# Sixteen experts in eight pairs of 64 slots, by plain float32 matmuls on weights as they come from memory

## The chip, the core and the metric

One core of a Trainium2 chip runs one program: a block with a state-space mixer, attention and a mixture of experts, and behind it a block of two layers with three kinds of attention, cross-attention and a feed-forward part. The metric is the device time of one execution in microseconds, as the median of runs. The engines named here are TensorE (PE in the profile; PEld is its loading of stationary operands), VectorE (DVE), ScalarE (ACT), GpSimd (POOL) and SyncE (SP), which issues nearly all loads.

## The reference

Only the mixture of experts matters. There are 256 tokens of 1024 features, four groups of four experts with 512 hidden features each, and all of it is float32. A token goes to the two best experts of its best group.

```python
g_prob = softmax(t @ w_rg + b_rg); g_p, g_idx = top_k(g_prob, 1)
e_in = (logits of the four experts of that group)
top_l, top_i = top_k(e_in, 2); w_k = softmax(top_l) * g_p
for e in range(16):
    hid = silu(t @ w_gate[e]) * (t @ w_up[e])       # [256, 1024] @ [1024, 512]
    out = out + gates[:, e:e+1] * (hid @ w_down[e])  # [256, 512] @ [512, 1024]
x = layer_norm(ALPHA * x + (1 + gt2) * out, ln2_g, ln2_b)
```

The weights of the experts are 16 x 3 matrices of 1024 x 512 float32, 2.10 MB each.

## The kernel before

Every large product takes float32 operands as two parts of type float32r, a higher and a lower one, and makes three matmuls of them (`mm3`, lines 159 to 163: high by high, high by low, low by high). Activations are split once. Weights come through `raw` (line 113: a buffer of 8 KB per partition, six in turn, loaded on SP's queue), and `wparts1` (line 128) splits them: a cast by ScalarE to the higher part and a subtraction by VectorE to the lower part, both in `split` at line 226, into two sets of four buffers of 4 KB (`hi` and `lo`).

`moe` (line 1038) norms the tokens, transposes and modulates them (`h2T`), and makes the router's logits (`plog`, line 1057; `lg`, line 1067). VectorE picks group and experts by a chain of small operations. The ranks of the tokens in their group come from matmuls with a strictly triangular matrix (line 1074), and from the ranks a one-hot matrix `S` of tokens by slots, 128 slots for each of the four groups (line 1094). Expert 0 takes every token, which gives TensorE work while the slots are made (`linB`, then `linA` with `dense`, lines 1130 to 1165). A branch for a group with more than 128 tokens stands between these two.

`gather` (line 1212) multiplies the normed tokens with `S`, so that each slot gets its token, feature-major. `experts` (line 1268) then goes through fifteen jobs, one for each remaining expert, each over the 128 slots of its group: gate and up (`pgu`, 24 matmuls each), silu and product (lines 1306 and 1307), four transposes (line 1322), and down (`yg`, 24 matmuls). A group's sum is brought back to its tokens by `combine` (line 1351) with the transposed one-hot matrix. The gate of the next expert is written between the steps of the one before. Which instruction comes when on each engine is set by a scheduler before the run, in order of the source as far as operands are there by its reckoning; on the chip each engine keeps that order. `after` puts instructions behind given ones.

Behind the experts follow a layer norm and the second block. Keys and values of its second memory (`keys`, `values`) fill TensorE during that norm. The first memory's values (`self.values(0, ...)`) fill the router's time.

Of the kernel before, what the change touches and what calls it, by code (L numbers as in the profile page):

```python
# [16 lines left out]
P = 128  # L17
# [37 lines left out]
KCST = NCST - 4 * P     # without the identity in front and the masks behind  # L55


def bc(ap, axis, n):
    """insert a broadcast dimension of n at axis"""
    u = ap.unsqueeze(axis)  # L60
    shape = list(u.shape)
    shape[axis] = n
    return u.to_broadcast(shape)


class Build:
# [75 lines left out]
    def wblk(self, src, a, b, r=None, pages=None):  # L142
        """a block of weights [128, a, b], split into its two parts: pairs of [128, b]. r: loaded before"""
# [7 lines left out]
    def wpages(self, src, a, b):  # L151
        """the same by way of pages alone; and these, to be freed"""
# [63 lines left out]
    def linB(self, x, KT, W, n0, r=None, w=None):  # L216
        """feature-major (x @ W[:, n0:n0+256])^T: a bank [128, 2, 256]"""
# [10 lines left out]
    # feature-major activations in two parts: pages of four feature tiles [128, 4, 256]  # L228
# [11 lines left out]
    def featT(self, src, KT, xT, t):  # L240
        """transpose the token-major src [128, KT*128] of token tile t into xT"""
# [10 lines left out]
    def rsq(self, src, mul, eps, n, name):  # L252
        """(src*mul + eps) ** -0.5"""
# [13 lines left out]
    def square(self, sq, n, x, out=None):  # L267
        """half n of the sum of squares of x [128, 1024]; sq: a page for the squares, a column for each half"""
# [8 lines left out]
    def rms1(self, sq, r):  # L277
        """r = (the mean of the squares + eps) ** -0.5"""
# [6 lines left out]
    def norm1(self, sq, x, g, r=None):  # L285
        """the page of sq gets the rms-normed x with its gain"""
# [7 lines left out]
    def normT(self, x, gain, name, sq=None, eng=None, r=(None, None)):  # L294
        """rms-normed x with its gain, transposed, in two parts. sq: the squares, where they are summed already"""
# [7 lines left out]
        self.chain = []     # the splits, in their order  # L303
# [28 lines left out]
    def lngb(self, out, v, st, g, b, then):  # L332
        """out = layer norm of v with gain and bias, by halves; then(n): called after each"""
# [40 lines left out]
    def ptile(self, pr, nh, n, eng):  # L374
        """the nh*n transposes [128 keys, nh, n, 128 queries] of the probabilities pr [128, nh, n*128]"""
# [13 lines left out]
    def attn(self, qk, V, out, first=True, nsink=None, gate=None, swa=False):  # L389
        """Causal attention of four heads over 256 tokens, added to out [128, 2, 256] (pairs of heads on  # L390
# [317 lines left out]
    def mixer1(self):  # L708
# [155 lines left out]
        for m in mods:  # L864
            self.modend(m)
# [987 lines left out]
```

## Time and profile before

| | |
|---|---|
| median of three runs | 1766.82 us (1764.88 to 1770.11) |
| the profiled execution, from its first to its last instruction | 1764.4 us |
| TensorE busy | 1686.6 us (96%) |
| VectorE busy | 1216.9 us (69%) |
| ScalarE busy | 940.7 us (53%) |
| read from memory | 337.85 MB, 192 GB/s over the span |
| router, first expert, fifteen experts, tail of the experts | 381 to 718 us |

A busy TensorE is not one at its peak: matmuls overlap, and their ends are modelled. What a matmul costs in a stream is the distance from one start to the next, not its duration.

### The profile page before, as it was taken

To read this page: it belongs to the slowest core of one execution; us is meant where nothing else is said; L and a number is where in the kernel's file an instruction comes from. 1 tells how busy PE (TensorE), PEld (TensorE's weight loads), DVE (VectorE), ACT (ScalarE), POOL (GpSimd) and SP (SyncE) were. 2 spreads that over 40 slices of the span, in tenths; PEclk is the share of its full clock that TensorE was granted. 3 is DMA by queue.
4 is the path that set the end of the run, shared out by engine and by line. 5 is a ranking of instruction groups with operands and counts; after the bars stand their busy time and mean duration, and the time that the engine had idled before them with its cause. 6 is when DMAs were issued, how large, how long until landed. Compare 5 with 4: busy or idle time off the path is not lost. (4 is left out here: it accounts for less than half of the span.)

```text
span 1764.4 us, 25175 instructions
## 1 busy us (share of the span) xinstructions
PE 1686.6 (96%) x9802; PEld 1420.9 (81%) x9818; DVE 1216.9 (69%) x1724; ACT 940.7 (53%) x1497; POOL 233.4 (13%) x260
## 2 busy tenths in 40 slices
PE   6699999999999999999999999999999999999998
PEld 5579888887888877786778779998777778789986
DVE  6856875886899988777754765554677746755543
ACT  3346754455777776566554455443575544544442
POOL 3589245120000000200000000000100000000000
PEclk9699999989999999999999999999999999999999
DMA  9867366545899989453335635654453255535550
GB/s 313 293 199 229 96 227 238 167 168 163 314 312 370 354 316 367 147 190 88 114 114 188 205 108 179 196 181 150 140 170 98 72 168 202 182 129 173 186 191 24
DMA packets 206845, 340.60 MB, mean 193 GB/s; under 512 B 19792, under 2 KB 99776, under 8 KB 206720
## 3 DMA queue, kind: packets, MB, share of 16 engines
q1 hardware_dynamic: 202864, 331.29, 56.0%
q0 software_dynamic: 1936, 6.52, 1.1%
q8 instruction: 79, 1.29, 0.3%
q10 hardware_dynamic: 1920, 1.11, 0.2%
q14 instruction: 46, 0.38, 0.1%
HBM read 337.85 MB, written 1.05 MB: 192 GB/s over the span
## 5 line engine op out<-in xcount | busy, mean ns | idle before, releaser
L226 DVE TENSOR_TENSOR wlo<-raw,whi 128x1024 fp32r<-128x1024 f32 (+3 forms) x560 | 680.0, 1232 | 340.3 <-ACT whi L226 334.5
L226 ACT CAST whi<-raw 128x1024 fp32r<-128x1024 f32 (+3 forms) x560 | 568.8, 1031 | 461.8 <-PE psA L163 167.3
L161 PE MATMUL psB<-hTh,whi 128*128 128x256 f32 x896 | 255.3, 285 | 0.9 <-DVE xbc L859 0.9
L163 PE MATMUL psB<-hTh,wlo 128*128 128x256 f32 x896 | 255.1, 285 | 0.8 <-DVE wlo L226 0.8
L162 PE MATMUL psB<-hTl,whi 128*128 128x256 f32 x896 | 255.3, 285 | 0.0
L161 PE MATMUL psA<-whi,hTh 128*128 128x512 f32 (+4 forms) x496 | 187.9, 379 | 2.6 <-ACT sg L950 1.9
L163 PE MATMUL psA<-whi,hTl 128*128 128x512 f32 (+4 forms) x496 | 187.4, 378 | 0.5 <-DVE hTl L226 0.5
L162 PE MATMUL psA<-wlo,hTh 128*128 128x512 f32 (+4 forms) x496 | 186.3, 376 | 0.0
L161 PEld LDWEIGHTS psB<-hTh,whi 128*128 128x128 f32 x896 | 171.6, 192 | 3.7 <-DVE xbc L859 1.8
L162 PEld LDWEIGHTS psB<-hTl,whi 128*128 128x128 f32 x896 | 171.3, 191 | 1.9 <-issue 1.9
L163 PEld LDWEIGHTS psB<-hTh,wlo 128*128 128x128 f32 x896 | 171.4, 191 | 1.7 <-DVE wlo L226 1.1
L161 PEld LDWEIGHTS psA<-whi,hTh 128*128 128x128 f32 x496 | 93.7, 189 | 20.8 <-ACT sg L950 2.3
L163 PEld LDWEIGHTS psA<-whi,hTl 128*128 128x128 f32 x496 | 93.5, 188 | 19.0 <-issue 2.4
L162 PEld LDWEIGHTS psA<-wlo,hTh 128*128 128x128 f32 x496 | 93.6, 189 | 16.1 <-issue 0.7
L162 PE MATMUL pgu<-wlo,gh 128*128 128x512 f32 x240 | 96.0, 400 | 2.2 <-DVE wlo L226 2.0
L361 ACT ACTIVATE pr<-S,nm 128x256 f32<-128x256 f32 (+1 forms) x160 | 66.3, 425 | 59.5 <-DVE nm L354 41.8
L161 PE MATMUL pgu<-whi,gh 128*128 128x512 f32 x240 | 95.6, 399 | 0.0
L163 PE MATMUL pgu<-whi,gl 128*128 128x512 f32 x240 | 94.7, 395 | 0.0
L633 POOL TENSOR_TENSOR macc<-macc,wmod 128x512 f32<-128x512 f32 x59 | 92.6, 1571 | 1.8
L162 PE MATMUL pd<-wlo,hhl 128*128 128x512 f32 x176 | 69.7, 396 | 0.0
L163 PE MATMUL pd<-whi,hhl 128*128 128x512 f32 x176 | 69.5, 395 | 0.0
L161 PE MATMUL pd<-whi,hhl 128*128 128x512 f32 x176 | 69.2, 395 | 0.0
(595 smaller groups left out, 3248.1 us busy)
## 6 DMA issues: line engine op xcount, KB each, us to landing
raw<-in_w_in SPq DMA_DIRECT2D x62, 1024.0 KB, 5.1
raw<-in_w_down SPq DMA_DIRECT2D x52, 1024.0 KB, 5.9
raw<-in_w_gate_up SPq DMA_DIRECT2D x44, 1024.0 KB, 5.1
raw<-in_w_gate SPq DMA_DIRECT2D x32, 1024.0 KB, 6.4
raw<-in_w_up SPq DMA_DIRECT2D x32, 1024.0 KB, 6.5
wmod<-in_w_mod SPq DMA_DIRECT2D x48, 512.0 KB, 5.5
raw<-in_w_xkv SPq DMA_DIRECT2D x8, 1024.0 KB, 9.6
raw<-in_w_out SPq DMA_DIRECT2D x8, 1024.0 KB, 5.0
```

Of the source, the lines that this page charges most:

```text
L161: m(out, l[0], r[0], start=start, stop=False)
L162: m(out, l[0], r[1], start=False, stop=False)
L163: self.lastmm = m(out, l[1], r[0], start=False, stop=stop)
L226: return self.nc.scalar.copy(hi, src), self.nc.vector.tensor_sub(lo, src, hi.bitcast(F32))
L361: le = nc.scalar.activation(pr[:, h, :], S[:, h, :], AF.Exp, bias=nm[:, h:h + 1], accum_out=den[:, h:h + 1])
L633: return e.tensor_add(acc, acc, w)
```

## The change

An expert has 64 slots instead of a group 128. Ranks and one-hot matrix are made for each of the 16 experts, after the choice of experts. Two experts make a pair. Expert 2q has the first 64 columns of TensorE's array and expert 2q + 1 the last 64, so that their results stand on partitions 0 to 63 and 64 to 127 of one PSUM bank. The operands are plain float32: the weights are used as they are loaded, without parts. Features are assigned to partitions in another order, partition p holding features 8p to 8p + 7, so that a partition reads 8 KB of a weight matrix in one piece; the modulation of the second norm, the transposes and the router's weights follow that order. A chunk of weights (1 MB) goes to a `raw` buffer or to a pair of `hi` and `lo` buffers in turn. All sixteen experts go this way, expert 0 too. If an expert has more than 64 tokens, a branch between pairs 3 and 4 multiplies all tokens by all experts with the gates of those that found no slot. The second memory's load and the first split of its weights are issued behind the last load of the experts.

The diff, cut to its core:

```diff
+    CHUNKS = "rrhrh"
+    def wchunk(self, src):
+        n, b = src.shape[1:]
+        kind = self.CHUNKS[self.nchunk % len(self.CHUNKS)]
+        self.nchunk += 1
+        if kind == "r":
+            r = self.raw(src, n, b)
+            return [r[:, k * b:(k + 1) * b] for k in range(n)]
+        out = []
+        for h, tag in enumerate(("hi", "lo")):
+            m = n // 2
+            t = self.wp.tile([P, 1024], F32, tag=tag, bufs=self.HL, name="wx")
+            v = t.rearrange("p (a b) -> p a b", a=m)
+            self.lastraw = self.nc.sync.dma_start(v, src[:, h * m:(h + 1) * m, :])
+            out += [v[:, k, :] for k in range(m)]
+        return out
...
+            nc.tensor.matmul(pk[:, t * 16:t * 16 + 16], self.stri, sf[:, t, :], start=True, stop=t == 0, skip_group_check=True)
+        nc.tensor.matmul(pk[:, 16:32], self.ones, sf[:, 0, :], start=False, stop=True, skip_group_check=True)
...
+            nc.vector.tensor_tensor(Sp[t].rearrange("p (e s) -> p e s", e=16), bc(self.iota[:, 0:64], 1, 16), bc(rr[:, t, :], 2, 64), op=ALU.is_equal)
...
+        for b in range(2):
+            for k in range(8):
+                ps = self.bank("o" if k % 2 else "tp", "pga")
+                for t in range(2):
+                    r = Sp[t][:, b * 512:(b + 1) * 512]
+                    for n, v in enumerate((xh, xl)):
+                        nc.tensor.matmul(ps, v[t].rearrange("p (q k) -> p k q", k=8)[:, k, :], r, start=t == 0 and n == 0, stop=t == 1 and n == 1)
...
-        W = [A[n][0, 0] for n in ("w_gate", "w_up", "w_down")]
-        hid = [self.glu(self.linB(self.T(h2), 8, W[0], b * 256), self.linB(self.T(h2), 8, W[1], b * 256)) for b in range(2)]
...
-        self.experts(jobs, acc, st=st, ahead=first, early=early, more=pair(1), fin=mem)
+        wgu = lambda j, e, c: W[j][e].rearrange("(p k) n -> p k n", k=8)[:, 4 * c:4 * c + 4, :]
+        wdn = lambda e, c: W[2][e].rearrange("(p j) n -> p j n", j=4)[:, 2 * c:2 * c + 2, :]
+        def half(q, j):
+            ps = self.bank("lin", "pgu")
+            for c in range(2):
+                w = ready.pop(0) if ready else [self.wchunk(wgu(j, 2 * q + i, c)) for i in range(2)]
+                for k in range(4):
+                    kt = 4 * c + k
+                    for i in range(2):
+                        x = xg[q // 4][kt // 2][:, kt % 2, q % 4 * P + i * 64:q % 4 * P + i * 64 + 64]
+                        self.lastmm = nc.tensor.matmul(ps[i * 64:i * 64 + 64, :], x, w[i][k], start=kt == 0, stop=kt == 7, skip_group_check=True)
+            return ps
...
+        for q in range(8):
+            if q == 4:
+                ready += [[self.wchunk(wgu(0, 8 + i, c)) for i in range(2)] for c in range(2)]
+                self.overflow(oi, hT, gov, acc)
+                self.f(*hT, *xgp[0])
+            pg, pu = half(q, 0), half(q, 1)
+            if late:
+                self.combine(ST[(q - 1) // 4][:, (q - 1) % 4, :], evac(late), acc)
+            hid = self.a(2, "hid")
+            nc.scalar.activation(hid, pg, AF.Silu)
+            nc.vector.scalar_tensor_tensor(hid, hid, gs[:, q:q + 1], pu, op0=ALU.mult, op1=ALU.mult)
+            pt = v4(self.bank("m", "pth"))
+            for k in range(4):
+                nc.tensor.transpose(pt[:, k, :], hid.rearrange("p (f k) -> p k f", k=4)[:, k, :], self.ident)
+            hx = self.a(2, "hx")
+            nc.scalar.copy(v4(hx), pt)
+            y = [self.bank("S", f"yg{n}") for n in range(2)]
+            for c in range(2):
+                w = [self.wchunk(wdn(2 * q + i, c)) for i in range(2)]
+                for k in range(2):
+                    for n in range(2):
+                        for i in range(2):
+                            nc.tensor.matmul(y[n][i * 64:i * 64 + 64, :], v4(hx)[:, 2 * c + k, i * 64:i * 64 + 64], w[i][k][:, n * 512:(n + 1) * 512],
+                                             start=c == 0 and k == 0, stop=c == 1 and k == 1, skip_group_check=True)
+            self.f(hid, hx)
+            late = y
+        with self.after(self.lastraw):
+            mT = self.memT(1)
+            w = self.wB(8, A["w_xkv_2"][1], 0)
+        self.combine(ST[1][:, 3, :], evac(late), acc, st)
...
+    def overflow(self, oi, hT, gov, acc):
+        flag = nc.values_load(oi[0:1, 0:1], min_val=0, max_val=1)
+        with self.tc.If(flag > 0):
+            for e in range(16):
...
+                                nc.tensor.matmul(ps[t], v4(hT[k // 4])[:, k % 4, t * P:(t + 1) * P], wv[:, k - k0, :], start=k == 0, stop=k == 7)
```

## Rows read from the trace of the kernel before

**Rows 1.** The page: busy time, share of the span and instructions of each engine.
```profile
PE 1686.6 (96%) x9802; PEld 1420.9 (81%) x9818; DVE 1216.9 (69%) x1724; ACT 940.7 (53%) x1497; POOL 233.4 (13%) x260
```
**Rows 2.** Windows: stretch, length; PE, PEld, DVE, ACT, POOL busy; clock, DMA share, GB/s.
```profile
340.00:381.00 41.00, 37.90 (x171) 31.39 (x170) 33.34 (x45) 16.88 (x27) 14.65 (x12) 0.79 0.42 138
381.00:427.00 46.00, 41.68 (x289) 38.46 (x289) 31.30 (x79) 24.43 (x31) 0.00 (x0) 0.96 0.53 176
427.00:704.00 277.00, 274.01 (x1231) 219.61 (x1229) 251.82 (x266) 205.88 (x230) 2.24 (x4) 1.00 0.93 332
...
440.00:460.00 20.00, 20.00 (x90) 16.11 (x89) 18.30 (x17) 15.35 (x17) 0.00 (x0) 1.00 0.71 256
```
**Rows 3.** Stationary loads for gate and up's PSUM tile: ns min/median/max.
```profile
L161 PEld LDWEIGHTS pgu<-whi,gh x240: 187/188/192, 427.0 to 689.3; 128*128 128x128 f32 x120
```
**Rows 4.** Waits of the SP queue, 430 to 705 us: total, times, longest.
```profile
SPq L116 <- DVE wlo L226: 226.7, 81, 8.8
```
**Rows 5.** Groups of instructions, 427 to 704 us: busy us, mean ns.
```profile
L226 DVE TENSOR_TENSOR wlo<-raw,whi 128x1024 fp32r<-128x1024 f32 x172 | 203.9, 1221 | 15.3 <-ACT whi L226 13.9
L226 ACT CAST whi<-raw 128x1024 fp32r<-128x1024 f32 x173 | 177.9, 1051 | 50.4 <-PE pgu L163 28.6 <-PE yg L163 18.5 <-ACT hf L1229 0.6
...
L1307 DVE SCALAR_TENSOR_TENSOR hid<-hid,gs,pgu 128x512 f32<-128x512 f32 x15 | 11.1, 743 | 0.2 <-PE pgu L163 0.2
```
**Rows 6.** Timeline, a plain float32 matmul of attention scores: start, us, instruction.
```profile
811.33 1.02 PE L424 MATMUL S<-kaD,qaT 128*128 128x512 f32 x2
```
**Rows 7.** Timeline, the attention's value products, 64 columns wide.
```profile
795.56 0.27 PE L414 MATMUL oT<-PT,vm 128*64 128x128 f32 x1
795.57 0.27 PE L413 MATMUL oT<-PT,vm 128*64 128x128 f32 x1
795.67 0.27 PE L415 MATMUL oT<-PT,vm 128*64 128x128 f32 x1
```
**Rows 8.** DMA view of three saturated windows: 92 to 100, 66 to 76, 601 to 607 us.
```profile
DMA packets 2767, 2.79 MB, mean 348 GB/s; under 512 B 46, under 2 KB 2767, under 8 KB 2767
...
DMA packets 2000, 3.86 MB, mean 386 GB/s; under 512 B 116, under 2 KB 116, under 8 KB 2000
...
DMA packets 738, 2.43 MB, mean 405 GB/s; under 512 B 45, under 2 KB 45, under 8 KB 737
```
**Rows 9.** Timeline of the router: VectorE's chain, TensorE's ranks, ScalarE's last copy of values.
```profile
378.78 0.59 ACT L1711 COPY vx<-psA 128x512 f32<-128x512 f32 x1 [0.55 <-PE psA L163]
...
382.07 0.19 DVE L1067 TENSOR_TENSOR lg<-plog,rb 128x40 f32<-128x40 f32 x1
...
383.50 0.17 DVE L1026 TENSOR_TENSOR oh<-lg,gm 128x8 f32<-128x8 f32 x1
...
384.10 0.17 DVE L1030 TENSOR_TENSOR oh<-oh,ohm 128x8 f32<-128x8 f32 x1
...
384.42 0.57 PE L1074 MATMUL prank<-oh,cst 128*128 128x4 f32 x4
...
385.70 0.17 DVE L1079 SCALAR_TENSOR_TENSOR rr<-prank,oh 128x8 f32<-128x8 f32 x1 [0.97 <-PE prank L1077]
```
**Rows 10.** Timeline of TensorE: the gates of the slots and the transposed one-hot.
```profile
422.69 0.95 PE L1242 MATMUL pgs<-wg,S 128*128 128x4 f32 x8
423.50 0.42 PE L1250 MATMUL pst<-idt,S 128*128 128x128 f32 x2
```
**Rows 11.** Timeline of TensorE at the branch, and the window behind it.
```profile
409.88 0.47 PE L161 MATMUL psA<-whi,hhl 128*128 128x512 f32 x1 [4.12 <-PEq L1144]
...
410.00:415.00 5.00, 5.00 (x16) 3.93 (x17) 0.53 (x1) 0.00 (x0) 0.00 (x0) 0.66 0.63 203
```
**Rows 12.** Timeline of the tail: the last expert matmul, a split, the last statistics.
```profile
701.99 0.39 PE L163 MATMUL yg<-whi,hl 128*128 128x512 f32 x1
...
707.88 1.22 DVE L226 TENSOR_TENSOR wlo<-raw,whi 128x1024 fp32r<-128x1024 f32 x1
...
716.34 1.28 DVE L312 BATCH_NORM_STATS2 bst<-acc 128x6 f32<-128x512 f32 x2
```

More of the change, by code (lines that the diff above doesn't have):

```diff
@@ L672, in mod, with modendq @@
         return list(self.modsteps(j))[-1]
+    def modendq(self, ja):
+        j, acc = ja
+        ps = self.bank("m", "psmod")
+        mm = self.nc.tensor.matmul
+        mm(ps[:, 0:8], self.ident, self.bq[:, j - 3, :], start=True, stop=False, skip_group_check=True)
+        for k in range(8):
+            mm(ps[:, k:k + 1], acc.rearrange("p (q k) -> p k q", k=8)[:, k, :], self.ones[:, 0:1], start=False, stop=True, skip_group_check=True)
+        if j == 4:
+            self.nc.vector.tensor_scalar(self.modq[:, 1, :], ps[:, 0:8], 1.0, None, op0=ALU.add)
+        else:
+            self.nc.scalar.copy(self.modq[:, 0, :], ps[:, 0:8])
+        self.f(acc)
     def modend(self, ja):
@@ L863, in mixer1 @@
         Bf, Cf = v4(xp[2]), v4(xp[3])
[L864 to L865 removed]
+        self.modend(mods[0])
+        self.modendq(mods[1])
         with self.after(self.lastraw):
@@ new lines, in moe @@
+        ov = self.small([P, 2, 16], "ov", 1)
+        nc.vector.tensor_scalar(ov, rr, 63.5, None, op0=ALU.is_ge)
+        of = self.small([P, 1], "of", 1)
+        nc.vector.tensor_reduce(of, ov.rearrange("p t e -> p (t e)"), axis=AX.X, op=ALU.add)
+        pf = self.bank("o", "pof")
+        nc.tensor.matmul(pf[:, 0:1], self.ones, of, start=True, stop=True)
+        oi = self.cp.tile([1, 1], I32, name="oi")
+        nc.vector.tensor_scalar(of[0:1], pf[0:1, 0:1], 1.0, None, op0=ALU.min)
+        nc.vector.tensor_copy(oi, of[0:1])
@@ new lines, in moe @@
+        self.behind = self.behind0
+        self.values(0, self.mT0)
+        self.freeT(self.mT0)
+        Sf = [v.bitcast(F32) for v in Sp]
+        pg = self.bank("m", "pgs")
+        for q in range(8):
+            for t in range(2):
+                nc.tensor.matmul(pg[:, 2 * q:2 * q + 2], Sf[t][:, q * P:(q + 1) * P], g16[:, t, 2 * q:2 * q + 2], start=t == 0, stop=t == 1,
+                                 skip_group_check=True)
+        gs = self.small([P, 8], "gs", 1)
+        for i in range(2):
+            c = slice(i * 64, (i + 1) * 64)
+            nc.vector.tensor_copy(gs[c, :], pg[c, 0:16].rearrange("p (q i) -> p q i", i=2)[:, :, i])
@@ new lines, in moe @@
+        STp = [self.a(4, f"ST{i}", F32R) for i in range(2)]
+        ST = [v4(v) for v in STp]
+        for i in range(2):
+            for t in range(2):
+                pt = v4(self.bank("m", "pst"))
+                for q in range(4):
+                    nc.tensor.transpose(pt[:, q, :], Sf[t][:, (4 * i + q) * P:(4 * i + q + 1) * P], self.ident)
+                nc.scalar.copy(ST[i][:, :, t * P:(t + 1) * P], pt)
+        xg = [[self.a(4, f"xg{b}{i}").rearrange("p (a b) -> p a b", a=2) for i in range(4)] for b in range(2)]
@@ L1130, in moe @@
         self.mod_tm(5, gt)
-        self.behind = self.behind0
-        self.values(0, self.mT0)
-        self.freeT(self.mT0)
-        W = [A[n][0, 0] for n in ("w_gate", "w_up", "w_down")]
-        hid = [self.glu(self.linB(self.T(h2), 8, W[0], b * 256), self.linB(self.T(h2), 8, W[1], b * 256)) for b in range(2)]
-        self.freeT(h2)
-        ahead = [self.raw(W[2][:, n * 512:(n + 1) * 512].rearrange("(k p) n -> p k n", p=P), 4, 512) for n in range(2)]
-        first = [self.raw(*self.wsrc(A[n][0, 1], k0)) for n in ("w_gate", "w_up") for k0 in (0, 4)]
@@ L1186, in moe @@
-        list(pair(0))
-        st = self.newst()
-        mT, w = [], []
-        def mem():
-            with self.after(self.lastraw):
-                mT.extend(self.memT(1))
-                w.extend(self.wB(8, A["w_xkv_2"][1], 0))
-        self.experts(jobs, acc, st=st, ahead=first, early=early, more=pair(1), fin=mem)
+        st = self.newst()
+        self.nchunk = 0
+        W = [A[n][0] for n in ("w_gate", "w_up", "w_down")]
+        wgu = lambda j, e, c: W[j][e].rearrange("(p k) n -> p k n", k=8)[:, 4 * c:4 * c + 4, :]
@@ L1235, in slots @@
-    def slots(self, S, wg, ng):
-        nc = self.nc
-        Sf = S.bitcast(F32)
-        pg = self.bank("m", "pgs")
-        for g in range(ng):
-            for t in range(2):
-                nc.tensor.matmul(pg[:, g * 4:g * 4 + 4], Sf[:, t, g, :], wg[:, t, :], start=t == 0, stop=t == 1)
-        gs = self.small([P, ng, 4], "gs")
-        nc.vector.tensor_copy(gs, pg[:, 0:4 * ng].rearrange("p (a b) -> p a b", a=ng))
-        STp = self.a(ng, "ST", F32R)
-        ST = STp.rearrange("p (g t) -> p g t", g=ng)
-        for t in range(2):
-            pt = self.bank("m", "pst").rearrange("p (a b) -> p a b", a=4)
-            for g in range(ng):
-                nc.tensor.transpose(pt[:, g, :], Sf[:, t, g, :], self.ident)
-            nc.scalar.copy(ST[:, 0:ng, t * P:(t + 1) * P], pt[:, 0:ng, :])
-        return gs, STp
@@ L1362, in combine, with glu @@
         self.f(*y[0], *y[1])
+    def glu(self, pg, pu):
+        h = self.a(2, "hid")
+        hv = h.rearrange("p (a b) -> p a b", a=2)
+        self.nc.scalar.activation(hv, pg, AF.Silu)
+        self.nc.vector.tensor_mul(hv, hv, pu)
+        hl = self.a(4, "hhl", F32R)
+        self.split(hl[:, 0:512], hl[:, 512:1024], h)
+        self.f(h)
+        return hl
     def rope(self, dst, src, t, H, w=64):
```

295 lines of the change are left out of this document (105 added, 190 removed).

## The prediction

> **What bounds the kernel now.** I read the page's shares first, then a table of windows around the mixture of experts, then single instructions. TensorE is busy for 96% of the span [rows 1], so at first sight it is the bound everywhere. The table of windows [rows 2] divides the part that changes: the router and the first, dense expert (381 to 427 us), fifteen experts of 128 slots (427 to 704 us) and the tail (704 to 718 us). In the 277 us of the experts TensorE is busy for 274 us at the full clock (2.4 GHz), and the DMA engines are busy for 0.93 of the time as well, at 332 GB/s. Two limits lie almost on each other here. In 20 us of it 90 matmuls of 512 columns start [rows 2], one per 0.222 us. An expert has 72 of them (gate and up 8 k-tiles each, down 4 k-tiles in two halves, three passes), 16.0 us, and 6.29 MB of weights, which at 332 GB/s is 18.9 us; 277 / 15 = 18.5 us is what one really takes. The SP queue, which issues the weights, waited 227 us for VectorE's lower parts of the weights to free a buffer [rows 4]: the loads are asked for only as fast as the splits and matmuls use them.
>
> **What is removed.** All weight splits of the stage go: 172 subtractions, 204 us of VectorE, and 173 casts, 178 us of ScalarE [rows 5]. Neither engine is the bound, so by themselves they are worth nothing; they matter because a buffer no longer waits for them. What both still do for a pair (silu, product, four additions, the splits of the result, some 6 us each at 0.6 to 0.75 us for an operation on 512 columns [rows 5]) lies beside 20 us and more of other work. The 1080 split matmuls of the fifteen experts (240 us), the dense expert's matmuls in 381 to 423 us and the first fillers go too.
>
> **What TensorE gets instead.** Per pair of experts: gate and up, 2 x 8 k-tiles x 2 experts, and down, 4 k-tiles x 2 halves x 2 experts, 48 plain float32 matmuls of 512 columns, each 64 columns of the array wide. What such a matmul costs stands in another stage: a plain float32 matmul of 512 columns leaves two records in 1.02 us, the second starting some 0.43 us behind the first (1.02 less the 0.60 that one record takes by itself) [rows 6]. So 96 records per pair, 41 us if they run one after the other. The attention's value products are the same kind, 64 columns wide on the two halves of PSUM's partitions, and their records start in twos, 10 ns apart, with 0.11 us between the twos [rows 7], at 128 columns a quarter of 0.43. The two halves do run together. So I take 96 x 0.43 / 2 = 20.6 us per pair. With four transposes (0.6 us) and the eight matmuls that return the rows (1.8 us) it is 23 us, and some 25 us with the wait between up and down for silu, product and copy; 41 + 2.4 = 43 us stays the upper bound.
>
> **What the DMA gets.** The bytes stay: 16 x 3 x 2.10 MB = 100.7 MB, 12.6 MB per pair. At 23 to 25 us TensorE would ask for 500 GB/s or more. No window shows that, so the supply becomes the bound and its rate is the main term. Saturated windows show how the rate goes with the packet [rows 8]: 348 GB/s at about 1.0 KB, 386 at 1.9 KB, 405 at 3.3 KB a packet (megabytes by packets). Before, gate and up come in rows of 2 KB. The change reads 8 KB in one piece for each partition where a chunk takes a raw buffer and 4 KB where it takes a pair of smaller ones, three to two. A line through time per packet (2.9, 5.0 and 8.1 ns) has 2.3 to 2.4 ns per KB and puts 8 KB near 420 GB/s, an estimate. I take 405, the largest that a window shows, for a supply that is never quite without gaps; 348 and 420 are the ends for the range.
>
> The Trainium skill gives about 358 GB/s as HBM's limit for one core (DMA: Bandwidth & Descriptors, Specifications). The trace does not hold to it, with 405 GB/s in a window; by that rule the stage would need 90.2 / 0.358 = 252 us and the time would be 1729 us.
>
> **When the supply starts to matter.** Ten chunks fit into the buffers (six raw, four pairs), 10.5 MB. They can load while the router works, when the DMA is half idle (0.42 and 0.53 of the time [rows 2]). The third chunk takes small buffers that the splits for the cross-attention's values hold until those end, at 379 us [rows 9], and on SP everything behind it waits; the 8.4 MB from there on need 21 us at 405 GB/s, to 400 us. So all ten are there, and 90.2 MB remain when the first chunk is freed. The logits are ready at 382 us. Twenty small VectorE operations at 0.20 us (three from 383.50 to 384.10), the ranks on TensorE and the wait for them, 1.3 us, two more operations, 0.4 us, and two one-hot tiles of 1024 columns at 1.2 us as a subtraction of that size [rows 5, 9] give 390.5 us. Then TensorE has 32 records for the gates (0.12 us each), 16 transposes (0.15 us by pairs) [rows 10], together 6.2 us, and 64 gather matmuls of 512 columns at 0.23 us, 15 us: 412 us if the experts begin behind all of it, 404 us if they begin behind the first half. The first two chunks are free 3.4 us later (16 records by twos): 407 to 415 us. I take 411.
>
> The gather reads its stationary rows eight elements apart, which no row of before does. It costs nothing if the load hides behind a matmul as the others do (a gain is excluded, since they hide already), and I bound it by a second load of 0.19 us each [rows 3], 64 x 0.19 = 12 us. I take nothing, as the nearest rows are loads that hide, and keep the 12 us for the range. The Trainium skill says that SBUF wants two hits on a line of 16 bytes and that a read pays otherwise (SBUF — State Buffer, Door 1: The DMA port swizzle). No run here shows that yet.
>
> The other edits (shift and scale of the second norm in another order of features, 9 small matmuls for 10; one small load at the start on ScalarE's queue) have one answer: they stand in the mixer, far ahead of their use, and I cost them at nothing; uncovered they would be under 2 us.
>
> **The branch.** The old one stopped TensorE for 4.12 us and left the clock at 0.66 for the next 5 us [rows 11]. The new one stands between pairs 3 and 4 with four chunks issued ahead. TensorE has 31 - 25 = 6 us to spare in each pair, so it is covered as long as the supply is the bound; without that cover it costs some 6 us. SP pays it too, with up to ten chunks under way (26 us), which covers it as well.
>
> **The sum.** 411 + 90.2 / 0.405 = 411 + 223 = 634 us for the last byte. Then the last chunks' matmuls, 3.4 us, and the return to tokens: before, the last statistics end 15.6 us after the last expert matmul (702.0 to 717.6) with some 4 us of splits between them [rows 12], so 12 us here: 649 us against 717.6, 68.6 us less. The second memory's load now stands behind the last weights instead of beside them; keys and values (22 us of TensorE) then reach some 2 us beyond the layer norm that they fill. So 66.6 us off. The profiled execution spans 1764.4 us and the runs' median is 1766.8, 2.4 more; I take the 66.6 from the median: 1700 us.
>
> **Rivals.** (a) *The supply is slower.* For: the stage's mean is 332 GB/s now [rows 2]. Against: those gaps are waits for buffers [rows 4]. At 348 GB/s, the rate of packets of 1 KB, the 90.2 MB take 259 us: 1736 us. The limit that the Trainium skill gives, above, would be a milder form of this case. (b) *TensorE sets the pace, at 43 us per pair*, because the halves don't overlap at 512 columns, or because waits for chunks leave the clock at its lower level, 1.2 GHz. For: the overlap is seen at 128 columns alone, and the clock did fall after 4 us without work [rows 11]. Against: the rows are even over all heads, the waits expected here are under 2 us (5.2 us for the bytes of two chunks less 3.4 us for their matmuls), and a slow TensorE stops waiting. 404 + 8 x 43 + 15 = 763 us, 45 us later than now: 1812 us, slower. It decides from (717.6 - 404 - 15) / 8 = 37 us per pair on. (c) *The branch is taken.* It reads all experts again and multiplies 16 x 96 records at full width, 0.43 us each, 660 us: 2360 us. It decides when an expert has more than 64 tokens. The routing worked out from the reference and its inputs at the default seed gives 63 for the fullest expert and 32 on the mean, so it isn't taken, by two tokens.
>
> **How the numbers follow.** The forecast 0.72, (a) 0.15, (b) 0.07, (c) 0.03, and 0.03 for stalls that eat the gain. The forecast's own spread: 8 us less at 420 GB/s, 4 us either way for the start, 5 us for the tail, 12 us more for the gather: 1683 to 1718 us. The range takes in (a) and a little beyond either end: 1677 to 1742. Faster by over 0.3% (about what a measurement of this kernel can tell from no change): 0.72 + 0.15 + 0.01 = 0.88; same 0.02; slower 0.10.
>
> **What the profile after would show.** Right: expert records starting in twos 0.43 us apart; TensorE busy for about 0.75 of the stage and waiting for raw chunks; DMA share near 1.0 at about 405 GB/s; no splits; the first expert matmul near 404 us and the last statistics near 649. Wrong: records that start one at a time, a granted clock of 0.5 in the stage, a DMA rate under 350, a first expert far behind 412 us, or instructions of the overflow.

## The result, and the profile after

The change runs in 1710.1 us (median of 4 runs, 1708.2 to 1711.8) against 1765.9 us for the kernel before (median of 4, one run more than ahead of the prediction), a ratio of 0.9687 (95% interval 0.9668 to 0.9706). The forecast was 1700 us, with 1677 to 1742 as its range. The gain is 56 us where 66.6 were forecast.

First the page's busy line, as in [rows 1], and then windows over the stage, as in [rows 2] (stretch, length; PE, PEld, DVE, ACT, POOL busy; clock, DMA share, GB/s).

```profile
PE 1604.0 (94%) x9272; PEld 1263.8 (74%) x9288; DVE 987.6 (58%) x1497; ACT 736.7 (43%) x1278; POOL 232.5 (14%) x260
```

```profile
378.00:388.00 10.00, 4.73 (x24) 3.95 (x24) 8.07 (x40) 1.58 (x5) 1.04 (x1) 0.84 0.60 210
388.00:400.00 12.00, 12.00 (x57) 11.62 (x57) 0.98 (x5) 2.90 (x5) 0.00 (x0) 0.57 0.00 0
400.00:416.00 16.00, 16.00 (x69) 15.42 (x68) 5.30 (x7) 5.45 (x7) 0.20 (x1) 1.00 0.00 1
...
420.00:430.00 10.00, 10.00 (x49) 3.41 (x46) 0.00 (x0) 0.60 (x1) 0.00 (x0) 1.00 0.92 351
...
516.00:532.00 16.00, 12.68 (x54) 4.60 (x51) 4.55 (x7) 1.14 (x2) 0.63 (x1) 1.00 0.76 285
532.00:640.00 108.00, 93.46 (x376) 32.12 (x374) 18.47 (x28) 7.78 (x13) 0.00 (x0) 0.98 1.02 416
640.00:652.00 12.00, 9.79 (x41) 4.24 (x40) 2.73 (x5) 1.20 (x2) 0.55 (x1) 1.00 1.03 399
652.00:668.00 16.00, 12.21 (x76) 10.64 (x75) 15.54 (x25) 8.63 (x12) 0.74 (x2) 0.89 1.05 384
```

Three things stand in these rows. The supply is saturated at 416 GB/s and is the bound, though TensorE shows 93 of 108 us busy: two records of 0.59 us run at once, so that its busy share can't be read as need. The DMA engines stand still from 388 to 420 us, since all ten chunks have landed and no buffer is free; in that time TensorE gathers, at first at a granted clock of 0.57. And the supply dips to 285 GB/s at 516 to 532 us, around the branch.

VectorE's chain of [rows 9] ends with the one-hot tiles, at 387.4 us:

```profile
385.02 2.36 DVE L1146 TENSOR_TENSOR S<-cst,rr 128x1024 fp32r<-128x1024 f32 x2
```

What SP's queue does and waits for from 416 to 655 us answers to [rows 4] (the first line is from its timeline, the others give total, times and longest wait):

```profile
419.80 0.81 SPq L116 DMA_DIRECT2D raw<-in_w_down  x2
...
SPq L116 <- PE pgu L1237: 26.2, 6, 22.9
SPq L1077 <- DMA raw<-in_w_up: 20.4, 10, 2.3
```

No split is left among what it waits for, where 227 us of waits stood before. The longest wait, 22.9 us, is the one for TensorE to free the first buffer. Over the whole stretch some 48 us are waits for TensorE and 140 us, in pieces of at most 4 us like those of the last line, are waits for an earlier load of its own to land.

The pairs' matmuls in TensorE's timeline (start, us, instruction) answer to [rows 6, 7]: they start in twos, 0.43 us from two to two.

```profile
420.04 0.59 PE L1237 MATMUL pgu<-wx,xg 128*64 128x512 f32 x1
420.04 0.59 PE L1237 MATMUL pgu<-raw,xg 128*64 128x512 f32 x1
420.46 0.59 PE L1237 MATMUL pgu<-wx,xg 128*64 128x512 f32 x1
420.47 0.59 PE L1237 MATMUL pgu<-raw,xg 128*64 128x512 f32 x1
```

The tail in the timeline answers to [rows 12]: the last expert matmul ends at 650.8 us and the last statistics at 665.3, 52 us earlier than before. Another 3.4 us came off behind it, to make the 55.6 us between the two profiled spans (1764.4 and 1708.8 us).

```profile
649.82 1.02 PE L1273 MATMUL yg<-raw,hx 128*64 128x512 f32 x2
...
650.02 0.69 DVE L1244 TENSOR_TENSOR yf<-yg,gt 128x512 f32<-128x512 f32 x1 [8.39 <-PE yg L1273]
...
655.87 0.68 DVE L1244 TENSOR_TENSOR yf<-yg,gt 128x512 f32<-128x512 f32 x1
...
664.05 1.28 DVE L312 BATCH_NORM_STATS2 bst<-acc 128x6 f32<-128x512 f32 x2
```

### The profile page after: what moved, and what is told of

The parts are those of the page before. It is cut to its first block, busy times and chain, and to the rows that moved or that the text cites. A ratio compares the mean times of both kernels' runs of the same rounds, so it can differ in the third digit from the quotient of the medians.

```text
span 1708.8 us, 23523 instructions
## 1 busy us (share of the span) xinstructions
PE 1604.0 (94%) x9272; PEld 1263.8 (74%) x9288; DVE 987.6 (58%) x1497; ACT 736.7 (43%) x1278; POOL 232.5 (14%) x260
## 3 DMA queue, kind: packets, MB, share of 16 engines
HBM read 337.86 MB, written 1.05 MB: 198 GB/s over the span
## 5 line engine op out<-in xcount | busy, mean ns | idle before, releaser
L226 DVE TENSOR_TENSOR wlo<-raw,whi 128x1024 fp32r<-128x1024 f32 (+3 forms) x372 | 455.7, 1235 | 315.2 <-ACT whi L226 314.4
L226 ACT CAST whi<-raw 128x1024 fp32r<-128x1024 f32 (+3 forms) x372 | 375.2, 1021 | 381.1 <-PE psA L163 152.3
L1237 PE MATMUL pgu<-raw,xg 128*64 128x512 f32 x304 | 115.3, 600 | 6.0 <-DMA raw<-in_w_up 3.9
L1237 PE MATMUL pgu<-wx,xg 128*64 128x512 f32 x208 | 94.8, 600 | 0.4 <-DMA wx<-in_w_up 0.4
L1237 PEld LDWEIGHTS pgu<-raw,xg 128*64 128x64 f32 x304 | 34.1, 137 | 50.2 <-issue 37.2
```

The costliest lines, as they stand in the source:

```text
L226: return self.nc.scalar.copy(hi, src), self.nc.vector.tensor_sub(lo, src, hi.bitcast(F32))
L1237: self.lastmm = nc.tensor.matmul(ps[i * 64:i * 64 + 64, :], x, w[i][k], start=kt == 0, stop=kt == 7, skip_group_check=True)
```

## The experiments

The kernel's first 300 us move by some 4 us either way between profiled executions (in the change and its variants TensorE first loads the mixer's gate tile, `gTh`, between 300.4 and 308.8 us). Differences of a few microseconds are therefore read between marks inside the stage too: the logits `lg`, the first expert matmul, the last expert matmul, the last statistics (in us, to within 0.1). Times are medians; the ratio is that to the kernel before, measured in the same round (its medians were 1766.0, 1768.9 and 1769.4 us beside the runs named a, b and c).

| kernel | us | ratio, 95% interval | logits to last statistics | logits to first expert | first to last expert | last expert to statistics |
|---|---|---|---|---|---|---|
| before | 1765.9 | | 335.5 | 45.1 | 275.2 | 15.2 |
| the change | 1710.1 | 0.9687, 0.9668 to 0.9706 | 286.9 | 37.6 | 234.7 | 14.6 |
| a1_ahead8 | 1714.9 | 0.9708, 0.9665 to 0.9751 | 286.9 | 37.9 | 234.5 | 14.5 |
| a2_contig | 1713.0 | 0.9708, 0.9664 to 0.9751 | 284.4 | 36.1 | 234.3 | 14.0 |
| a3_rows2k | 1723.5 | 0.9770, 0.9723 to 0.9818 | 298.0 | 37.9 | 245.9 | 14.2 |
| a4_half | 1663.1 | 0.9419, 0.9378 to 0.9460 | 242.8 | 37.8 | 194.7 | 10.3 |
| b1_nobranch | 1704.6 | 0.9643, 0.9622 to 0.9664 | 280.0 | 37.7 | 227.8 | 14.5 |
| b2_early | 1705.2 | 0.9635, 0.9619 to 0.9651 | 279.5 | 13.3 | 251.7 | 14.5 |
| b3_warm | 1708.1 | 0.9651, 0.9630 to 0.9671 | 283.5 | 34.3 | 234.9 | 14.3 |
| b5_front | 1701.8 | 0.9616, 0.9599 to 0.9634 | 275.9 | 16.4 | 243.8 | 15.7 |
| c1_front | 1707.7 | 0.9656, 0.9632 to 0.9680 | 283.8 | 37.9 | 231.4 | 14.5 |
| c2_both | 1698.0 | 0.9597, 0.9573 to 0.9622 | 272.7 | 17.0 | 241.2 | 14.5 |
| c3_combine | 1716.7 | 0.9711, 0.9686 to 0.9737 | 281.5 | 37.8 | 235.9 | 7.8 |
| c4_serial | 1735.3 | 0.9811, 0.9773 to 0.9849 | 313.1 | 37.5 | 259.1 | 16.5 |

**What is the bound: half the bytes (a4_half).**

```diff
-                w = ready.pop(0) if ready else [self.wchunk(wgu(j, 2 * q + i, c)) for i in range(2)]
+                w = ready.pop(0) if ready else [self.wchunk(wgu(j, 2 * q, c))] * 2
...
-                ready += [[self.wchunk(wgu(0, 8 + i, c)) for i in range(2)] for c in range(2)]
+                ready += [[self.wchunk(wgu(0, 8, c))] * 2 for c in range(2)]
...
-                w = [self.wchunk(wdn(2 * q + i, c)) for i in range(2)]
+                w = [self.wchunk(wdn(2 * q, c))] * 2
```

> Both experts of a pair use the weights of the first one, loaded once: half the bytes, every matmul kept; the odd experts' own weights are left out. Theory (supply sets the pace): pairs come every 25 us, TensorE's own pace, in place of 29.3; 8 x 4.3 = 34 us less, time about 1676. Rival (TensorE sets the pace): no change, 1710.

The stage shrinks by 44 us and the time to 1663 us, more than the 34 us and 1676 us expected: 40 us lie between the first and the last expert matmul, and 4 behind it. ScalarE's timeline shows the pairs' pace (each pair has one silu), 24.5 us, and a window shows TensorE busy almost without a gap while only 266 GB/s flow.

```profile
449.09 0.60 ACT L1260 ACTIVATE hid<-pgu 128x512 f32<-128x512 f32 x1 [3.84 <-PE pgu L1237]
473.56 0.60 ACT L1260 ACTIVATE hid<-pgu 128x512 f32<-128x512 f32 x1 [4.70 <-PE pgu L1237]
498.02 0.60 ACT L1260 ACTIVATE hid<-pgu 128x512 f32<-128x512 f32 x1 [4.70 <-PE pgu L1237]
...
420.00:600.00 180.00, 178.74 (x800) 65.82 (x798) 44.34 (x67) 22.59 (x35) 1.52 (x3) 1.00 0.77 266
```

That is TensorE's own need, the 25 us of the forecast; a pair's bytes take 30.2 us at 416 GB/s. The rival in which TensorE sets the pace of the change falls.

**What the rate hangs on: rows of 2 and 4 KB (a3_rows2k).**

```diff
-        wgu = lambda j, e, c: W[j][e].rearrange("(p k) n -> p k n", k=8)[:, 4 * c:4 * c + 4, :]
-        wdn = lambda e, c: W[2][e].rearrange("(p j) n -> p j n", j=4)[:, 2 * c:2 * c + 2, :]
+        wgu = lambda j, e, c: W[j][e].rearrange("(k p) n -> p k n", k=8)[:, 4 * c:4 * c + 4, :]
+        wdn = lambda e, c: W[2][e].rearrange("(j p) n -> p j n", j=4)[:, 2 * c:2 * c + 2, :]
```

> The weights are read in the old order of features, in rows of 2 KB (gate, up) and 4 KB (down), the operands stay; so the products pair features with the wrong rows of the weights, the work is the same. Theory (supply sets the pace, and its rate hangs on the packet): near 386 GB/s in place of 416, 90.2/0.386 - 90.2/0.416 = 17 us more, time about 1727. Rival (TensorE sets the pace, it is busy for 93% of the stage): no change, 1710. Second rival (the rate doesn't hang on the packet): 416 GB/s as now, no change.

From first to last expert matmul it took 11.2 us more. The DMA view from 540 to 600 us, first of the change and then of this run, answers to [rows 8]:

```profile
DMA packets 4823, 25.00 MB, mean 417 GB/s; under 512 B 540, under 2 KB 540, under 8 KB 3006
```

```profile
DMA packets 10002, 23.67 MB, mean 395 GB/s; under 512 B 509, under 2 KB 509, under 8 KB 9999
```

90.2 MB at 395 and at 417 GB/s differ by 12 us; the 17 us expected took 386 GB/s, but down's rows, a third of the bytes, are of 4 KB here. Both rivals fall, and the other order of features pays for itself with these 11 us. The forecast's line through time per packet had put 8 KB near 420 GB/s.

The Trainium skill holds two figures for this. HBM's limit for one core, about 358 GB/s (DMA: Bandwidth & Descriptors, Specifications), by which the forecast had a milder rival of 1729 us, is not what these rows show. A core that streams alone reaches about 425 GB/s (HBM Reference, Specifications (TRN2)); with 417 GB/s this case agrees.

**The branch (a1_ahead8, b1_nobranch).** In the change's timeline of SP's queue nothing is issued between 507 and 523 us, and TensorE stops from 522.7 to 526.0.

```profile
507.08 0.33 SPq L116 DMA_DIRECT2D raw<-in_w_gate  x1
523.11 0.82 SPq L1077 DMA_DIRECT2D wx<-in_w_gate  x2
```

The first try issued more chunks ahead of it.

```diff
-                ready += [[self.wchunk(wgu(0, 8 + i, c)) for i in range(2)] for c in range(2)]
+                ready += [[self.wchunk(wgu(j, 8 + i, c)) for i in range(2)] for j in range(2) for c in range(2)]
```

> Gate and up of pair 4 (eight chunks) are issued ahead of the branch, not the gate alone. Theory (the loads set the pace, and SP stood at the branch until TensorE came to it, so that its queue ran dry): 516 to 532 us moved 285 GB/s where 416 is usual, 16 x (1 - 285/416) = 5.0 us; that dip goes and the time falls by 5 us, to about 1705. Rival (the branch costs what TensorE stands still, 3.9 us without a matmul before 526 us): that stop stays, the time stays at 1710.

It tells nothing of this, and is a repeat of the change (the stage took 286.9 us both times). In its timeline, as in that of the change, SP issues one chunk of the next gate ahead of the branch (at 511.89 us) and not four, and the next at 527.90 us. Why the others stand behind the branch was not shown; the scheduler placed them there before the run.

What SP waits for at line 1303, where the branch ends, is the same in both runs (total, times, longest):

```profile
SPq L1303 <- SPq L1303: 15.3, 4, 9.8
```

In the trace these are waits for the eight semaphores that count the landings of SP's loads, one after another. Four of them hold SP up, and the last ends at 522.76 us, 15.7 us behind the issue of the last load ahead of the branch (507.08 us). SP goes on only when every load under way has landed. Then the branch was left out.

```diff
-                self.overflow(oi, hT, gov, acc)
```

> The overflow branch is left out altogether (no expert has more than 64 tokens here). Theory (on SP the branch ends only when every load under way has landed, 15 us of queue, so the DMA engines run dry): the dip at 516 to 532 us goes, 16 x (1 - 285/416) = 5.0 us, time about 1705. Rival (the loads catch up elsewhere or TensorE has no room to use them): 1710, no change.

First to last expert matmul is 6.9 us shorter and the dip is gone; SP's timeline goes on through the same time, and the window moves 419 GB/s. The expected time, 1705 us, came.

```profile
506.94 0.33 SPq L116 DMA_DIRECT2D raw<-in_w_gate  x1
509.42 1.65 SPq L1077 DMA_DIRECT2D wx<-in_w_gate  x2
512.00 2.82 SPq L116 DMA_DIRECT2D raw<-in_w_gate  x2
...
516.00:532.00 16.00, 14.53 (x64) 5.30 (x62) 5.14 (x8) 1.16 (x2) 0.00 (x0) 1.00 1.02 419
```

The dip is 5.0 of the 6.9 us. Another 1.3 us come from a load of 0.5 MB on GpSimd's queue, the norm weights of the second memory. The change's branch holds it back to 524.8 us, when the DMA engines are full; without the branch it is issued at 416.6 us, when they are idle. In the change:

```profile
POOL gn L345 <- PEq L1303: 107.9, 1, 107.9
```

**The late start: the clock (b3_warm).** TensorE had little to do while VectorE picked the experts (4.73 of 10 us at 378 to 388). In TensorE's timeline 30 records of 2 columns for the gates then take 6.40 us. With idle matmuls put ahead they take 3.51.

```diff
+        with self.after(lastpl):
+            for _ in range(26):
+                nc.tensor.matmul(pw, xh[0][:, 0:P], xh[0][:, 512:1024], start=True, stop=True)
```

> 26 matmuls without use (float32r, 512 columns) stand between the router's logits and the ranks, where TensorE waited for VectorE from 379.9 to 386.3 us. Theory (that wait left the granted clock at 0.58 in 390 to 400 us, and the gates and transposes cost 11 us in place of 6.2): clock 1.0 there, gates 0.10 us apart in place of 0.20, 4 to 5 us less, time about 1705.5. Rival (the clock costs nothing that counts, or the added matmuls delay the ranks by as much): 1710.

The timeline of the change, then that of this run:

```profile
388.50 6.40 PE L1188 MATMUL pgs<-g,S 128*128 128x2 f32 x30
```

```profile
388.27 3.51 PE L1192 MATMUL pgs<-g,S 128*128 128x2 f32 x30
```

Clock 0.57 becomes 0.86 at 388 to 400 us, and the experts begin 3.3 us earlier behind the logits, all of which is still there at the last statistics. By the time alone (1708.1 against 1710.1) it could not be told.

**The late start: the strided loads (a2_contig).**

```diff
-            nc.scalar.copy(xh[t], xn)
-            nc.gpsimd.tensor_sub(xl[t], xn, xh[t].bitcast(F32))
+            pv = lambda v: v.rearrange("p (k q) -> p k q", k=8)
+            xv = xn.rearrange("p (q k) -> p k q", k=8)
+            nc.scalar.copy(pv(xh[t]), xv)
+            nc.gpsimd.tensor_sub(pv(xl[t]), xv, pv(xh[t].bitcast(F32)))
...
-                        nc.tensor.matmul(ps, v[t].rearrange("p (q k) -> p k q", k=8)[:, k, :], r, start=t == 0 and n == 0, stop=t == 1 and n == 1)
+                        nc.tensor.matmul(ps, v[t][:, k * P:(k + 1) * P], r, start=t == 0 and n == 0, stop=t == 1 and n == 1)
```

> The two parts of the normed tokens are stored with their features in the order in which the gather reads them, so that its stationary loads are contiguous. Theory (the strided load shows as 330 ns but hides for the most part): the distance of gather matmuls goes from 0.245 to the 0.21 to 0.22 us of other 512-column matmuls, 64 x 0.03 = 2 us, time about 1708. Rival (each strided load holds TensorE by its whole extra length, 0.14 us and more): 9 to 12 us, time about 1699. The reordered copies could cost ScalarE and GpSimd more, which would show ahead of 387 us.

The gather's tile, ns as min/median/max, in the change and then in this run:

```profile
L1211 PEld LDWEIGHTS pga<-S,xnh x32: 312/329/342, 387.4 to 415.3; 128*128 128x128 f32 x32
L1211 PE MATMUL pga<-S,xnh x32: 395/414/780, 387.5 to 415.5; 128*128 128x512 f32 x32
```

```profile
L1213 PEld LDWEIGHTS pga<-S,xnh x32: 186/187/337, 386.7 to 413.1; 128*128 128x128 f32 x32
L1213 PE MATMUL pga<-S,xnh x32: 387/397/775, 386.8 to 413.4; 128*128 128x512 f32 x32
```

A strided load takes 329 ns for 187, yet the experts begin only 1.5 us earlier behind the logits: it hides, but for a remainder. The reordered copies put the logits back by 3 us (from the mixer's first gate tile to the logits 74.3 us in the change, 77.4 here): ScalarE takes 2.14 us for each in place of 1.05, GpSimd 2.86 in place of 2.37. So nothing is won. That SBUF wants two hits on a line of 16 bytes (the Trainium skill, SBUF — State Buffer, Door 1: The DMA port swizzle) agrees with the longer load; what it costs here is the smaller number.

**The late start: begin before all tokens are gathered (b2_early).** The gather for pairs 4 to 7, the gates, the second gain and the transposed one-hot tiles move between the matmuls of pairs 0 to 3.

```diff
+        gather(0, range(8))
+        acc = self.x
...
+            pg = half(q, 0)
+            if q == 0:
+                with self.after(self.lastmm):
+                    gates()
+            pu = half(q, 1)
+            if q == 0:
+                with self.after(self.lastmm):
+                    self.mod_tm(5, gt)
+                    trans(0)
...
+            if q < 4:
+                gather(1, range(2 * q, 2 * q + 2))
```

> Pairs 0 to 3 begin behind the gather of their own tokens; the gather for pairs 4 to 7, the gates of the slots, the second modulation gain and the transposed one-hot tiles stand between the first pairs' matmuls, and the sums are kept in place of the input tokens. Theory (the loads set the pace, and the DMA engines stand idle from 388 to 421 us because no buffer comes free): the first chunk is freed some 10 to 17 us earlier and the end comes as much earlier, 1693 to 1700. Rival (TensorE has no room for the 20 us that move in between, 8 x 24.5 = 196 us of its own in 234): the end stays, 1706 to 1710.

The experts begin 24 us earlier, and SP's first new chunk is issued at 403 us in place of 420; the end comes only 7.4 us earlier. Windows of this run show why:

```profile
410.00:440.00 30.00, 30.00 (x137) 14.21 (x139) 4.38 (x8) 4.86 (x8) 0.00 (x0) 0.89 0.85 320
440.00:500.00 60.00, 57.07 (x226) 22.32 (x223) 14.89 (x22) 6.40 (x10) 0.00 (x0) 1.00 1.01 406
```

TensorE is busy without a gap there and frees buffers too slowly; the supply falls to 320 GB/s. 1705.2 us is nearer to the rival's 1706 than to the theory's 1700, and the rival is half right: gates, gain, transposes and a quarter of the gather in one pair make TensorE the bound for that pair.

**The three together (b5_front).** The edits are those of the two runs before and the branch's move that the next run shows, and the second gain moves ahead of the ranks:

```diff
+        gt = self.gt2 = self.a(4, "gt2")
+        with self.after(lastpl):
+            self.mod_tm(5, gt)
```

> The three together, with nothing left out: early first pairs as in the run before with the gain of the second modulation made in TensorE's wait ahead of the ranks, the gather's operand stored contiguously, and the overflow branch ahead of pair 0, where all ten chunks have landed. Theory (start, branch and gather add up, less 2 to 4 us that the branch stops TensorE at the start): 1710 - 13 - 5 - 1.5 + 3 = about 1693. Rival (TensorE becomes the bound, or the branch at the start costs as much as it saved): 1700 or more.

The rival's number came, 1701.8 us for its 1700 or more. The branch stops TensorE for 0.8 us where it stands inside the first gather:

```profile
397.37 0.47 PE L1201 MATMUL pga<-S,xnh 128*128 128x512 f32 x1 [0.79 <-PEq L1330]
```

The stage is 11.0 us shorter and not the 17 expected. The first pairs are still full (336 GB/s flow from 410 to 440 us), and the reordered copies again stand ahead of the logits (77.6 us from the gate tile); how the missing 6 us divide was not measured.

**The branch ahead of pair 0 (c1_front).** The added matmuls are those of b3_warm; the branch's move:

```diff
-            if q == 4:
-                ready += [[self.wchunk(wgu(0, 8 + i, c)) for i in range(2)] for c in range(2)]
+            if q == 0:
+                ready += [[self.wchunk(wgu(j, i, c)) for i in range(2)] for j in range(2) for c in range(2)]
                 self.overflow(oi, hT, gov, acc)
```

> The change, with 26 matmuls without use between logits and ranks and the overflow branch ahead of pair 0; nothing is left out. The stage is taken from the logits to the last statistics, since its beginning moves by some 4 us between executions: 286.9 us for the change, 280.0 without the branch, 283.5 with the added matmuls. Theory (ahead of pair 0 all loads have landed, so the branch costs next to nothing; 0.8 us of TensorE where it stood there): 286.9 - 7 - 3.3 + 0.8 = 277.4 us, time about 1700. Rival (the branch costs its 7 us wherever it stands): 283.5 us, 1707.

The rival's number came, by another way than it said. No load is lost (413 GB/s at 516 to 532 us), but right ahead of pair 0 TensorE has nothing else to do: it waits 3.68 us at the branch, and its first 16 records then take 5.23 us where the change needed 3.65 (granted clock 0.69 from 418.0 to 423.2 us, 1.00 in the change from 416 to 420).

```profile
417.99 5.23 PE L1241 MATMUL pgu<-raw,xg 128*64 128x512 f32 x16 [3.68 <-DVEq L1309]
```

Another 2 us from first to last expert matmul (231.4 against 227.8 without a branch, less the 1.6) stay unexplained.

**Both, spread out (c2_both).** Against b5_front, whose reordered copies are taken back, the core of the edit is:

```diff
-            pu = half(q, 1)
-            if q == 0:
+            if q == 1:
                 with self.after(self.lastmm):
                     trans(0)
+            if q in (2, 3):
+                with self.after(self.lastmm):
+                    gather(1, range(3 * q - 3, min(3 * q, 8)))
...
+            pu = half(q, 1)
...
-            if q < 4:
-                gather(1, range(2 * q, 2 * q + 2))
...
+            if q == 1:
+                gather(1, range(3))
```

> Early first pairs with the moved work spread (gates in pair 0, transposed one-hot tiles in pairs 1 and 4, the gather for pairs 4 to 7 in thirds over pairs 1 to 3), the second modulation gain made ahead of the ranks, the branch ahead of pair 0; the gather's operand as in the change; nothing is left out. Theory (the loads set the pace, TensorE has 30.2 - 24.5 = 5.7 us to spare in a pair, and what is moved there now fits): first chunk free near 402 us for 419.8, stage 286.9 - 16 - 6 = 265 us, time about 1690. Rival (TensorE is short of room, so that the loads pause again as at 410 to 440 us in the first try): stage 272 to 276 us, 1696 to 1701.

1698.0 us: the fastest that leaves nothing out, 12 us under the change, with intervals that don't overlap. The stage is 14.2 us shorter, the rival's number: 410 to 440 us now move 377 GB/s where b2_early moved 320, so TensorE is still short of room in the first pairs, only less.

```profile
410.00:440.00 30.00, 29.23 (x140) 11.87 (x141) 3.75 (x7) 4.40 (x8) 0.00 (x0) 0.94 0.98 377
```

**The tail (c3_combine).**

```diff
-        with self.after(self.lastraw):
+        keep = self.lastraw
+        self.combine(ST[1][:, 3, :], evac(late), acc, st)
+        self.f(*xgp[1], *STp)
+        with self.after(keep):
             mT = self.memT(1)
             w = self.wB(8, A["w_xkv_2"][1], 0)
-        self.combine(ST[1][:, 3, :], evac(late), acc, st)
-        self.f(*xgp[1], *STp)
```

> The last pair's return to the tokens is written ahead of the second memory's transposes and first weight split, not behind them. Theory (the 14.6 us from the last expert matmul to the last statistics, where 12 were forecast, are VectorE's, which makes the memory's norm and splits between the two halves of the return): 4 to 5 us less to the statistics, and the keys come later by as much; the layer norm is what the next mixer waits for, so 1 to 3 us off the time, about 1708. Rival (keys and values are then what TensorE lacks under the layer norm): no change, 1710, or slower.

The statistics come 5.4 us earlier behind the logits, but from the logits to the end of the span 1335.2 us pass where the change needs 1330.3. Windows show what is lost. In the change, and then in this run:

```profile
660.00:670.00 10.00, 8.61 (x64) 8.18 (x63) 9.65 (x16) 3.06 (x4) 2.12 (x2) 0.94 1.04 368
```

```profile
660.00:670.00 10.00, 5.83 (x26) 5.34 (x27) 10.00 (x16) 3.16 (x4) 0.25 (x1) 0.51 1.05 375
```

TensorE is busy for 5.8 of 10 us at a clock of 0.51, and VectorE for all of it. The memory's norm and splits have only moved behind the statistics, where VectorE is full with the layer norm, and TensorE waits for them to begin the keys: the second layer's first value products start 86 us behind the statistics, 76 in the change. The rival is right.

**Do the halves overlap by order? (c4_serial)**

```diff
-                for k in range(4):
-                    kt = 4 * c + k
-                    for i in range(2):
+                for i in range(2):
+                    for k in range(4):
+                        kt = 4 * c + k
```

(and the same for down.)

> The matmuls of a pair in another order: four k-tiles of expert 2q, then four of expert 2q + 1, in place of one of each in turn; operands, columns and loads are as in the change. Theory (the two column tiles overlap only where the matmuls alternate between them): records one at a time, 96 x 0.43 = 41 us and some 44 per pair, 8 x 44 - 234 = 118 us more, time about 1828, the case that was feared as rival (b). Rival (TensorE finds the other tile's matmul further back in its queue): no change, 1710.

Neither. The stage is 26 us longer, not 118. A run of a chunk's matmuls is now eight records of one expert and then eight of the other. In TensorE's timeline (records that follow each other closely are merged, x5 is five of them) the first four stand alone; then the other expert's first record starts beside the fifth, and from there the starts come in twos until the second eight have their last four left over:

```profile
458.41 2.36 PE L1237 MATMUL pgu<-raw,xg 128*64 128x512 f32 x5
460.18 0.64 PE L1237 MATMUL pgu<-wx,xg 128*64 128x512 f32 x1
460.61 0.59 PE L1237 MATMUL pgu<-raw,xg 128*64 128x512 f32 x1
460.66 0.59 PE L1237 MATMUL pgu<-wx,xg 128*64 128x512 f32 x1
...
461.47 0.59 PE L1237 MATMUL pgu<-raw,xg 128*64 128x512 f32 x1
461.52 2.31 PE L1237 MATMUL pgu<-wx,xg 128*64 128x512 f32 x5
```

If the scheduler kept the order of the edit, which was not read, TensorE takes up the other half's matmul while three records of the first expert are still to start, and does not keep the order of the program record by record there. Where one run of eight follows the next without a pause (447.4 to 454.1 us), all records start in twos; where other work or a wait stands between, four or eight stand alone at each end. Of the pairs' 768 records 196 start with no other within 0.15 us, where 98 do in the change. A pair takes 259.1 / 8 = 32.4 us, and 390 GB/s flow from 430 to 660 us. Longer runs of one half were not measured.

## Why the prediction was right, and where its sum was off

*The mechanism held.* With the splits gone SP no longer waits for them, TensorE needs 24.5 us per pair (25 forecast), and the supply sets the pace (a4, a3). Rival (b) had as its point of decision 37 us per pair; even the unfavourable order stays under it. Rival (c) didn't come: no instruction of the overflow ran.

*The terms, in the order of the sum.* From 649 us for the last statistics (forecast) to 665.3 (measured) are 16.3 us; the first five points make 16:

- **Start, 411 forecast, 419.8 measured.** The largest miss. The one-hot tiles were even earlier than taken (387.4 for 390.5), but the clock behind TensorE's wait (0.57 in the mean, mostly the level of 1.2 GHz) cost 3.3 us (b3), the strided loads 1.5 (a2), and 16 small matmuls of the second gain, which the sum had left out, some 2.3 (0.14 us each, between the gather's). The rest is the choice of the middle between 404 and 412 us: the scheduler began the experts behind all of the gather, the 412 end.
- **Supply, 223 us for 90.2 MB.** At 417 GB/s it is 216 us, 6 better than at the 405 taken.
- **Branch, nothing forecast, 6.9 us measured (b1).** This is the step that failed: "SP pays it too, with up to ten chunks under way (26 us), which covers it as well". What is under way is no cover, since the branch's end on SP waits for its landing; the queue is empty when SP goes on. Nor did four chunks stand ahead of it, as the forecast took: one did. That TensorE's stop (3.3 us) is covered by its spare time agrees with the sum, since the dip (5.0 us) and the load that was held back (1.3 us) leave only 0.6 us of the 6.9.
- **From first new load to last landing** 227.3 us passed (419.8 to 647.1, the last chunk's issue at 632.1 and 15.0 us); 216 and 6.9 leave 4 us. The slow first ten microseconds (351 GB/s) are 1.6 of them. The sum also took all bytes for weights of the experts: 91.6 MB moved in this time, 1.4 MB more than 90.2, some 3.4 us at 417 GB/s (the first of the second memory's loads, which share the engines with the last chunks, the norm weights that the branch held back, and instructions). 1.3 us of these stand with the branch above, so that 0.7 us of the 4 are left for the rest, too little to place.
- **Tail, 15.4 us forecast from the last byte, 18.2 measured.** VectorE makes the memory's norm and splits between the two halves of the return (650.0 and 655.9 us). It is no loss that another order gives back (c3).
- **Late keys, 2 us lost by forecast.** Not seen; 3.4 us were gained behind the statistics. From the statistics to the second layer's first value products 76.0 us passed before and 75.9 after, so it came later, where the change edits nothing. Its cause is open.

*The signs named ahead.* Twos 0.43 us apart, a DMA share near 1.0 and no splits: seen. The first expert matmul, near 404 by forecast, came at 416.1 us, for the reasons given under the start. TensorE busy for 0.75 of the stage: wrong as a sign, 0.87 (93.46 of 108 us), since overlapping records count for their full length; the need, 24.5 of 30.2 us, is 0.81.

*The range.* The measured 1710.1 us lies in the forecast's own spread, but the spread's upper end does not come out of its terms: 4, 5 and 12 us on 1700 make 1721, not 1718. That the total was off by 10 us only is in part luck: the supply's 6 us, the 3 us of the one-hot tiles and the 3.4 us behind the statistics went against the other misses.

## What to carry to other kernels

Where the loads are the bound, look for the time in which they can't be asked for: here 32 us ahead of the first freed buffer and 16 us of a silent queue at a branch, while TensorE's busy share looked full (0.79 to 1.00 in these windows). A conditional block costs what its end waits for, and that is read in the queue's waits; here it was cheap (0.8 us) only where nothing was under way and other work surrounded it. Before work is moved into an engine's spare time, count that time per step and spread the work so that no step gets more.

## What the runs showed of the hardware that was not expected

Matmuls on different column halves overlap even when the kernel's source puts eight records of one half ahead of eight of the other: the second eight begin beside the fifth of the first (c4: 32.4 us per pair, where one at a time would be some 45, the 41 us of 96 records at 0.43 and the 4 us that a pair takes beside them). A gate matmul of 2 columns takes 0.21 us at the clock after an idle stretch and 0.11 us without it (6.40 and 3.51 us for 30). The same branch stops TensorE for 0.8 us within the gather (b5) and for 3.7 us right ahead of the first pair (c1).
